# Tap work of a convolution pinned behind the newest weight load and conversion of its queue (hybrid MLA and Mamba-2 trunk, one core)

## The chip, the cores and the metric

The kernel runs on one core of one Trainium2 chip. The metric is device time in microseconds, the median of several runs. Engines are named as in the profile: PE is TensorE (PEld its weight loads), DVE is VectorE, ACT is ScalarE, POOL is GpSimd, and SP is the sync engine, which issues most DMAs.

## The reference, cut to what matters

Two layers: an MLA mixer with an MLP, and a Mamba-2 (SSM) mixer with an MLP, on 256 tokens of width 2048 in float32. The change touches only the SSM mixer:

```python
zxbcdt = h @ w_in                                  # 2048 x 10304
z, xbc, dt = split(zxbcdt)
xbc = silu(causal_depthwise_conv(xbc, conv_w, conv_b))   # width 4, along the tokens
xs, b_in, c_in = split(xbc)                        # 4096, 1024, 1024 channels
...
cb = einsum('blgn,bsgn->blsg', c_c, b_c)           # scores of a group, masked by decay
y_diag = einsum('blsgh,bsghp->blghp', cb[..., None] * decay, x_c)
y = (y_diag + d_skip * xs) * silu(z)               # then a norm per group, then @ w_out
```

There are 8 groups of 8 heads with 64 channels each. The convolution of the x part is `out[t] = sum_i w[i] * x[t - 3 + i] + b`, followed by `silu`.

## The kernel before, in words

**Weights.** All weights come from HBM as float32 in pieces of 128 x 1024 (a *unit*). Each unit is loaded by SP into a raw buffer (`wraw`, 6 buffers, `Flow.fetch`, L87). It is then split into two halves of reduced precision whose sum is the weight: ScalarE writes the high half `wh` (L102), and VectorE writes the low half `wl` as raw minus high (L103), each with 4 buffers. TensorE multiplies with both: for one unit 8 matmuls with `wh` (L325, L326) and then 4 with `wl` (L329). When TensorE's program comes to unit j, `Flow.next` has issued the loads up to j+6 and the conversions up to j+3. `self.last` is the newest high-half conversion that has been issued.

**Order.** `Trunk.block` walks over the keys of a product; one key is two units here, and after each key it calls `tick()`. A function registered with `later(n, fn)` runs at the (n+1)-th tick from then on; in this way the work around the products is spread over the keys. Only TensorE's queue runs in the order of this program. For the other engines and for SP a scheduler draws up the order at compile time with a cost model of its own, taking the program's order as priority among what it holds to be ready; each queue then runs strictly in that order on the chip, and an instruction that has to wait holds back all those behind it. `tc.issue_after(ins)` forces the instructions of a block to stand behind `ins` in the queue of their engine. Before the change only two places of the MLA layer use it.

**The SSM layer** runs its blocks in this order: `B0 d0 C0 x0 B1 x1 C1 x2 z0 x3 z1 x4 z2 o0 x5 z3 x6 z4 o1 x7 z5 z6 o2a z7 o2b o3`. An x block computes the 512 x channels of one group (4 keys, 8 units), a z block its gate, an o block part of the output product. Around them:

- `x_block(g)`: ScalarE copies the product out of PSUM into `x` (tile `xtm`, L1184), and a DMA from ScalarE's queue writes it to a DRAM tensor `xD` (L1185). `shift` reads it back from DRAM at three token offsets into `taps` (128 x 2 x 3 x 512, one buffer for all groups, L1191). `weights` loads the convolution weights and the bias, repeated over the partitions, into `cw` (one buffer, L1176). `mult(t)` multiplies the three shifted copies (L1195) and `x` itself (L1196) by their weights. L1196 overwrites `x`, so it has to wait until the write to `xD` has read it. `total(t)` adds the three taps and the bias (L1200) and then lets ScalarE take a tanh (L1202); `silu(t)` finishes with L1205. t is 0 or 1, one half of the tokens.
- `ahead` hands the group's 8 heads to a queue and starts `across` (two ticks later, L1219, L1221), the part of the second token half that comes from the first. It is the only reader of columns 128 to 255 of `cb[g]`.
- `cb_group(g)`: the scores of a group; VectorE masks the two diagonal parts (L1167), ScalarE copies the unmasked far part (L1168).
- `head`: the decay rows of a head come as `cm` from DRAM (L1246), go through ScalarE (L1250, L1251) and VectorE (L1253); after eight heads the products follow (L1268), then L1271 and L1273 on GpSimd and L1274 on VectorE.
- `z_block`: a tanh (L1288), L1289 on VectorE, then `gate`: L1299 on GpSimd, squares with sums on ScalarE (L296), and L1305 on VectorE.

Of the kernel before, what the change touches and what calls it, by code (L numbers as in the profile page):

```python
# [20 lines left out]
F32 = mybir.dt.float32  # L21
F32R = mybir.dt.float32r
I32 = mybir.dt.int32
AF = mybir.ActivationFunctionType
ALU = mybir.AluOpType
# [3 lines left out]
P = 128  # L29
# [42 lines left out]
class Flow:  # L72
# [8 lines left out]
    def fetch(self, ld, cuts=None, beside=None):  # L81
        n = ld.src.shape[-1]
        ld.tile = self.pools[ld.pool].tile([P, 1024], F32, tag=ld.pool, name=f"w{ld.pool}{self.loaded}")
        for o, z in cuts or ((0, n),):
            if cuts:
                beside()
            self.nc.sync.dma_start(ld.tile[:, o:z], ld.src[:, o:z])  # L87

    def load(self, upto, cuts=None, beside=None):
        while self.loaded < min(upto, len(self.units)):  # L90
# [4 lines left out]
    def halves(self, raw, n, step=None):  # L95

        nc = self.nc
        h = self.pools["wh"].tile([P, 1024], F32R, tag="wh", name=f"wh{self.done}")
        lo = self.pools["wl"].tile([P, 1024], F32R, tag="wl", name=f"wl{self.done}")
        for o in range(0, n, step or n):  # L100
            v = slice(o, o + (step or n))
            self.last = nc.scalar.activation(h[:, v], raw[:, v], AF.Copy)  # L102
            nc.vector.tensor_tensor(lo[:, v], raw[:, v], h[:, v].bitcast(F32), ALU.subtract)  # L103
        return h, lo

    def narrow_halves(self, raw):
# [63 lines left out]
def seven(layer, p, src):  # L170
# [9 lines left out]
    def unit(flow, name, d):  # L180
# [5 lines left out]
        def make():  # L186
            if name == "N7":
                add("b22", "b12", "b22")
                out = halves("b22")
                if d in LATE5:  # L190
                    nc.gpsimd.dma_start(st["b12"].tile, quarter(d, 0, 0), accum_op=ALU.add)
                return out
            if name == "N5" and d not in LATE5:
                add("b12", "b11", "b12")
                return halves("b12")
            if name == "N6":
                add("b11", "b11", "b22")
                out = halves("b11")
                nc.gpsimd.dma_start(st["b11"].tile, quarter(d, 1, 0), accum_op=ALU.add)  # L199
                return out  # L200
            return halves({"M1": "b11", "N4": "b11", "N5": "b12"}.get(name, name))
# [13 lines left out]
class Trunk:  # L215
# [822 lines left out]
    def ssm_body(self, sp, dp, gain):  # L1038
        nc, d, cst = self.nc, self.d, self.cst
# [23 lines left out]
        taps = sp.tile([P, 2, 3, 512], F32, name="taps")  # L1063
        xD = dp.tile([S + 3, GROUPS * 512], F32, name="xD")
# [5 lines left out]

        self.later(1, zeros)

        def conv(ev, ct, dst, lag):

            def half(j):
                b = self.bank(early[0])
                for k in range(2):
                    for t in range(2):
                        o = k * 256 + t * P
                        nc.tensor.transpose(b[:, o:o + P], ev[t][:, (2 * j + k) * P:(2 * j + k + 1) * P], self.ident)  # L1080
                a = self.scratch()
                for k in range(2):
                    c = ct + 2 * j + k
                    wc = lambda i: cst[:, C_CW + 4 * c + i:C_CW + 4 * c + i + 1]
                    s, o = b[:, k * 256:(k + 1) * 256], a[:, k * 256:(k + 1) * 256]
                    nc.scalar.activation(o, s, AF.Identity, bias=cst[:, C_CB + c:C_CB + c + 1], scale=wc(3))
                    for i in (2, 1, 0):
                        m = 3 - i
                        nc.vector.scalar_tensor_tensor(o[:, m:256], s[:, 0:256 - m], wc(i), o[:, m:256], ALU.mult, ALU.add)
                th = self.scratch()  # L1090
                nc.scalar.activation(th, a, AF.Tanh, scale=0.5)
                nc.vector.scalar_tensor_tensor(dst(j), th, 1.0, a, ALU.add, ALU.mult)
            self.later(lag, lambda: half(0))
            self.later(lag + 1, lambda: half(1))
# [9 lines left out]
        def bc_block(name, i):  # L1104
            accs = self.block([("si", name, i, q) for q in range(4)], xT)
            t = self.ktile(self.k4, F32)
            fm[name, i] = t
            conv(evac(accs), (32 if name == "B" else 40) + 4 * i,
                 lambda j: t[:, 2 * j:2 * j + 2].rearrange("p a b -> p (a b)"), 0)
# [50 lines left out]
        def cb_group(g):  # L1160
            B, C = fm["B", g // 4][:, g % 4], fm["C", g // 4][:, g % 4]
            b = self.bank(early[0])
            nc.tensor.matmul(b[:, 0:256], B[:, 0:P], C, start=True, stop=True)
            nc.tensor.matmul(b[:, 256:384], B[:, P:256], C[:, P:256], start=True, stop=True)
            t = sp.tile([P, 384], F32, tag="cb", name=f"cb{g}", bufs=5)
            for o in (0, 256):
                nc.vector.scalar_tensor_tensor(t[:, o:o + P], b[:, o:o + P], 0.125, tri[:, 0:P], ALU.mult, ALU.mult)  # L1167
            nc.scalar.activation(t[:, P:256], b[:, P:256], AF.Copy, scale=0.125)  # L1168
            cb[g] = t

        def x_block(g):
            cw = []

            def weights():
                cw.append(sp.tile([P, 2560], F32, tag="cw", name=f"cw{g}", bufs=1))
                nc.sync.dma_start(cw[0], d["cwx"][g])  # L1176

            self.later(2, weights)
            accs = self.block([("si", "x", g, q) for q in range(4)], xT)
            xt = sp.tile([P, 2, 512], F32, tag="xtm", name=f"xtm{g}", bufs=3)  # L1180
            x = [xt[:, t] for t in range(2)]
            th = [None, None]
            for t in range(2):
                nc.scalar.activation(x[t], accs[t], AF.Copy, scale=rs[t])  # L1184
            nc.scalar.dma_start(xD[3:S + 3, g * 512:g * 512 + 512].rearrange("(t p) n -> p t n", t=2), xt)  # L1185

            def shift():
                for t in range(2):
                    v = xD[t * P:t * P + P, g * 512:g * 512 + 512]
                    row = v.ap[0][0]  # L1190
                    nc.sync.dma_start(taps[:, t], bass.AP(tensor=v.tensor, offset=v.offset, ap=[[row, P], [row, 3], [1, 512]]))  # L1191

            def mult(t):
                flat = taps[:, t].rearrange("p i n -> p (i n)")
                nc.vector.tensor_tensor(flat, flat, cw[0][:, :1536], ALU.mult)  # L1195
                nc.vector.tensor_tensor(x[t], x[t], cw[0][:, 1536:2048], ALU.mult)  # L1196

            def total(t):
                for v in (taps[:, t, 2], taps[:, t, 1], taps[:, t, 0], cw[0][:, 2048:]):
                    nc.vector.tensor_tensor(x[t], x[t], v, ALU.add)  # L1200
                th[t] = self.scratch()
                nc.scalar.activation(th[t], x[t], AF.Tanh, scale=0.5)  # L1202

            def silu(t):
                nc.vector.scalar_tensor_tensor(x[t], th[t], 1.0, x[t], ALU.add, ALU.mult)  # L1205

            def ahead():
                xg[g] = x
                dg = self.gain_tile(d["dsk"][g])
                for i in range(8):  # L1210
                    hq.append((g, i, dg))
                heads_of = lambda v: v.rearrange("p (h f) -> p h f", h=8)
                spread = lambda v: v[:, 8 * g:8 * g + 8].unsqueeze(2).to_broadcast([P, 8, 64])
                xw = self.scratch()
                nc.gpsimd.tensor_tensor(heads_of(xw), heads_of(x[0]), spread(edge[:, 0]), ALU.mult)

                def across():
                    b = self.bank(False)
                    nc.tensor.matmul(b, cb[g][:, P:256], xw, start=True, stop=True)  # L1219
                    far[g] = sp.tile([P, 512], F32, tag="far", name=f"far{g}", bufs=2)  # L1220
                    nc.vector.tensor_tensor(heads_of(far[g]), heads_of(b), spread(edge[:, 1]), ALU.mult)  # L1221

                self.later(1, across)

            self.later(1, shift)
            if g >= 4:
                self.later(0, lambda: cb_group(g))
            self.later(3, lambda: mult(0))
            self.later(4, lambda: total(0))
            self.later(5, lambda: mult(1))  # L1230
            self.later(6, lambda: (silu(0), total(1)))
            self.later(7, lambda: (silu(1), ahead()))

        def pump():
            for _ in range(2 if len(hq) > HEAD_BACKLOG else 1):
# [316 lines left out]
```

## Time and profile before

| | |
|---|---|
| median of 3 runs | 2320.58 us (2319.15 to 2321.26) |
| profiled execution | 2318.87 us, span 2317.1 us |
| granted TensorE clock, mean | 0.999 |
| busy in the span | PE 2291.6, DVE 1922.5, ACT 1387.8, POOL 198.5 us |

A line of the profile names the source line, the engine, the operation and `out<-in` with the names of the tiles; in square brackets stands how long the engine was idle before it and what ended that. A line of the waits reads: who waited, for whom, then microseconds in total, the number of times and the longest. SPq, ACTq and the like are the parts of the engines that issue DMAs.

### The profile page before, as it was taken

What the parts mean: (1) busy time and instruction counts of PE and PEld (TensorE: products, weight loads), DVE (VectorE), ACT (ScalarE), POOL (GpSimd) and SP (SyncE); (2) the same over time, 40 slices, a digit from 0 to 9 for tenths busy, and PEclk for the clock granted to TensorE, in tenths of its full rate; (3) what the DMA queues carried; (4) which work ended last, traced back from release to release, by engine and by line L of the source; (5) the groups of instructions that cost most, each with busy time, mean ns of one, the idle gap of its engine ahead of it and who ended that gap; (6) DMA issues with size and microseconds to landing.
All of it is one profiled execution on the core that took longest, in us unless ns stands there. A gap on an engine that the chain in (4) does not pass through costs nothing. (4 is left out here: it accounts for less than half of the span.)

```text
span 2317.1 us, 30468 instructions
## 1 busy us (share of the span) xinstructions
PE 2291.6 (99%) x10929; PEld 1898.5 (82%) x10929; DVE 1922.5 (83%) x2318; ACT 1387.8 (60%) x1947; POOL 198.5 (9%) x229
## 2 busy tenths in 40 slices
PE   9999999999999999999989999999999999999999
PEld 8888888888888888888777877888888888888887
DVE  7776697899899897678888678676988989989885
ACT  7775466566666656564555555445666656666663
POOL 1430000000000000000121102011000000000000
PEclk9999999999999999999999999999999999999999
DMA  8444687887888878667777777766687788788875
GB/s 314 148 133 149 205 236 243 261 243 244 265 242 252 267 212 265 195 211 251 249 258 237 239 243 249 225 209 193 207 254 236 252 263 242 245 266 242 252 226 165
DMA packets 161912, 538.07 MB, mean 232 GB/s; under 512 B 17680, under 2 KB 26832, under 8 KB 160736
## 3 DMA queue, kind: packets, MB, share of 16 engines
q1 hardware_dynamic: 151264, 502.44, 66.2%
q0 software_dynamic: 8096, 29.41, 7.8%
q10 hardware_dynamic: 2400, 4.27, 0.5%
q8 instruction: 86, 1.41, 0.3%
q14 instruction: 66, 0.54, 0.1%
HBM read 529.65 MB, written 6.41 MB: 231 GB/s over the span
## 5 line engine op out<-in xcount | busy, mean ns | idle before, releaser
L102 ACT ACTIVATE wh<-wraw 128x1024 fp32r<-128x1024 f32 (+1 forms) x818 | 855.0, 1052 | 558.3 <-PE acc L326 215.6
L103 DVE TENSOR_TENSOR wl<-wraw,wh 128x1024 fp32r<-128x1024 f32 (+1 forms) x818 | 988.1, 1223 | 197.6 <-ACT wh L102 189.0
L594 PE MATMUL yp<-wh,k 128*128 128x512 f32 x896 | 350.1, 391 | 0.0
L595 PE MATMUL yp<-wl,k 128*128 128x512 f32 x896 | 349.2, 390 | 0.7 <-DVE wl L103 0.6
L596 PE MATMUL yp<-wh,k 128*128 128x512 f32 x896 | 349.1, 390 | 0.0
L325 PE MATMUL acc<-wh,xt 128*128 128x512 f32 x704 | 280.6, 399 | 4.0 <-ACT wh L102 4.0
L326 PE MATMUL acc<-wh,xt 128*128 128x512 f32 x704 | 275.3, 391 | 0.0
L102 ACT ACTIVATE wh<-wrx 128x1024 fp32r<-128x1024 f32 x168 | 177.9, 1059 | 136.8 <-PE yp L596 107.5
L103 DVE TENSOR_TENSOR wl<-wrx,wh 128x1024 fp32r<-128x1024 f32 x168 | 204.1, 1220 | 37.0 <-ACT wh L102 36.8
L329 PE MATMUL acc<-wl,xt 128*128 128x512 f32 x704 | 190.4, 392 | 10.1 <-DVE wl L103 10.0
L325 PE MATMUL acc<-wh,k 128*128 128x512 f32 x496 | 196.8, 397 | 2.3 <-ACT wh L102 2.2
L595 PEld LDWEIGHTS yp<-wl,k 128*128 128x128 f32 x896 | 168.3, 188 | 35.9 <-DVE wl L103 1.5
L596 PEld LDWEIGHTS yp<-wh,k 128*128 128x128 f32 x896 | 168.2, 188 | 35.0
L594 PEld LDWEIGHTS yp<-wh,k 128*128 128x128 f32 x896 | 168.3, 188 | 34.6
L326 PE MATMUL acc<-wh,k 128*128 128x512 f32 x496 | 193.4, 390 | 0.0
L594 PE MATMUL st<-wh,xt 128*128 128x512 f32 x448 | 177.0, 395 | 0.0
L595 PE MATMUL st<-wl,xt 128*128 128x512 f32 x448 | 174.9, 390 | 0.0
L596 PE MATMUL st<-wh,xt 128*128 128x512 f32 x448 | 174.9, 390 | 0.0
L329 PEld LDWEIGHTS acc<-wl,xt 128*128 128x128 f32 x704 | 131.6, 188 | 41.8 <-DVE wl L103 14.8
L325 PEld LDWEIGHTS acc<-wh,xt 128*128 128x128 f32 x704 | 132.9, 189 | 34.4 <-ACT wh L102 6.1
L326 PEld LDWEIGHTS acc<-wh,xt 128*128 128x128 f32 x704 | 133.0, 189 | 27.9 <-issue 1.2
L199 POOL DMA_DIRECT2D wrx<-mi x56 | 49.1, 876 | 1140.7 <-DVE wl L103 1034.6
(307 smaller groups left out, 3447.7 us busy)
## 6 DMA issues: line engine op xcount, KB each, us to landing
wraw<-mi SPq DMA_DIRECT2D x256, 512.0 KB, 5.2
wraw<-mo SPq DMA_DIRECT2D x256, 512.0 KB, 5.3
wraw<-si SPq DMA_DIRECT2D x160, 512.0 KB, 4.8
wraw<-so SPq DMA_DIRECT2D x64, 512.0 KB, 4.7
wrx<-mi SPq DMA_DIRECT2D x56, 512.0 KB, 5.4
wrx<-mi POOLq DMA_DIRECT2D x56, 512.0 KB, 8.2
wraw<-wo SPq DMA_DIRECT2D x32, 512.0 KB, 3.8
taps<-xD SPq DMA_DIRECT2D x16, 768.0 KB, 7.4
```

Source lines behind the costliest of these rows:

```text
L102: self.last = nc.scalar.activation(h[:, v], raw[:, v], AF.Copy)
L103: nc.vector.tensor_tensor(lo[:, v], raw[:, v], h[:, v].bitcast(F32), ALU.subtract)
L199: nc.gpsimd.dma_start(st["b11"].tile, quarter(d, 1, 0), accum_op=ALU.add)
L325: nc.tensor.matmul(accs[t][:, :n], ah, wh[:, q, :], start=first and kt + q == 0, stop=False)
L326: nc.tensor.matmul(accs[t][:, :n], al, wh[:, q, :], start=False, stop=False)
L329: nc.tensor.matmul(accs[t][:, :n], lhs(kt + q, t)[0], wl[:, q, :], start=False, stop=en and q == nk - 1)
L594: nc.tensor.matmul(b, ah, wh, start=first and q == 0, stop=False)
L595: nc.tensor.matmul(b, ah, wl, start=False, stop=False)
L596: nc.tensor.matmul(b, al, wh, start=False, stop=last and q == 1)
```

## The change

The new helper `behind(what)` opens `tc.issue_after` on the newest weight load (`last_load`), low-half conversion (`last_lo`) or high-half conversion (`last`) that has been issued. With it:

- the tap reads stand behind the newest weight load in SP's queue, and are registered one tick later; the load of `cw` is registered one tick later too
- the products of both token halves are registered for the same tick, behind the newest low-half conversion in VectorE's queue (before: ticks 4 and 6 after the block; now both at tick 5)
- the tanh becomes a function of its own, behind the newest high-half conversion in ScalarE's queue, at ticks 7 and 8 (before: with the sums, at ticks 5 and 7); the sums move from ticks 5 and 7 to 6 and 7, and both silu to tick 8
- the copy of the far score part runs one tick after its group's masked parts, behind the newest high-half conversion

No instruction is added or taken away.

```diff
-            self.nc.sync.dma_start(ld.tile[:, o:z], ld.src[:, o:z])
+            self.last_load = self.nc.sync.dma_start(ld.tile[:, o:z], ld.src[:, o:z])
...
-            nc.vector.tensor_tensor(lo[:, v], raw[:, v], h[:, v].bitcast(F32), ALU.subtract)
+            self.last_lo = nc.vector.tensor_tensor(lo[:, v], raw[:, v], h[:, v].bitcast(F32), ALU.subtract)
...
+        def behind(what):
+            return self.tc.issue_after(getattr(self.flow, what).ins)
...
-            nc.scalar.activation(t[:, P:256], b[:, P:256], AF.Copy, scale=0.125)
             cb[g] = t
+
+            def far_part():
+                with behind("last"):
+                    nc.scalar.activation(t[:, P:256], b[:, P:256], AF.Copy, scale=0.125)
+
+            self.later(0, far_part)
...
-            self.later(2, weights)
+            self.later(3, weights)
...
             def shift():
-                for t in range(2):
+                with behind("last_load"):
+                    for t in range(2):
...
             def mult(t):
                 flat = taps[:, t].rearrange("p i n -> p (i n)")
-                nc.vector.tensor_tensor(flat, flat, cw[0][:, :1536], ALU.mult)
-                nc.vector.tensor_tensor(x[t], x[t], cw[0][:, 1536:2048], ALU.mult)
+                with behind("last_lo"):
+                    nc.vector.tensor_tensor(flat, flat, cw[0][:, :1536], ALU.mult)
+                    nc.vector.tensor_tensor(x[t], x[t], cw[0][:, 1536:2048], ALU.mult)
...
             def total(t):
                 for v in (taps[:, t, 2], taps[:, t, 1], taps[:, t, 0], cw[0][:, 2048:]):
                     nc.vector.tensor_tensor(x[t], x[t], v, ALU.add)
+
+            def tanh(t):
                 th[t] = self.scratch()
-                nc.scalar.activation(th[t], x[t], AF.Tanh, scale=0.5)
+                with behind("last"):
+                    nc.scalar.activation(th[t], x[t], AF.Tanh, scale=0.5)
...
-            self.later(1, shift)
+            self.later(2, shift)
             if g >= 4:
                 self.later(0, lambda: cb_group(g))
-            self.later(3, lambda: mult(0))
-            self.later(4, lambda: total(0))
-            self.later(5, lambda: mult(1))
-            self.later(6, lambda: (silu(0), total(1)))
-            self.later(7, lambda: (silu(1), ahead()))
+            self.later(4, lambda: (mult(0), mult(1)))
+            self.later(5, lambda: total(0))
+            self.later(6, lambda: (tanh(0), total(1)))
+            self.later(7, lambda: (silu(0), tanh(1), silu(1), ahead()))
```

More of the change, by code (lines that the diff above doesn't have):

```diff
@@ L1187, in shift @@
             def shift():
-                for t in range(2):
-                    v = xD[t * P:t * P + P, g * 512:g * 512 + 512]
-                    row = v.ap[0][0]
-                    nc.sync.dma_start(taps[:, t], bass.AP(tensor=v.tensor, offset=v.offset, ap=[[row, P], [row, 3], [1, 512]]))
+                with behind("last_load"):
+                    for t in range(2):
+                        v = xD[t * P:t * P + P, g * 512:g * 512 + 512]
+                        row = v.ap[0][0]
+                        nc.sync.dma_start(taps[:, t], bass.AP(tensor=v.tensor, offset=v.offset, ap=[[row, P], [row, 3], [1, 512]]))
             def mult(t):
                 flat = taps[:, t].rearrange("p i n -> p (i n)")
-                nc.vector.tensor_tensor(flat, flat, cw[0][:, :1536], ALU.mult)
-                nc.vector.tensor_tensor(x[t], x[t], cw[0][:, 1536:2048], ALU.mult)
+                with behind("last_lo"):
+                    nc.vector.tensor_tensor(flat, flat, cw[0][:, :1536], ALU.mult)
+                    nc.vector.tensor_tensor(x[t], x[t], cw[0][:, 1536:2048], ALU.mult)
             def total(t):
```

## The prediction

> **What bounds the kernel now.** I read the page first, then the busy time by stage, then the waits, then the order of time around single stops. The page says that TensorE is the bound: it is busy for nearly the whole span, so only time in which it stands still can be won.
>
> ```profile
> span 2317.1 us, 30468 instructions
> ...
> PE 2291.6 (99%) x10929; PEld 1898.5 (82%) x10929; DVE 1922.5 (83%) x2318; ACT 1387.8 (60%) x1947; POOL 198.5 (9%) x229
> ```
>
> The next view cuts the SSM layer into stages. The three stages left out lost nothing. Columns: stage, its length, then the busy time of each engine, clock, DMA.
>
> ```profile
> core 0: us, PE busy (x) PEld busy (x) DVE busy (x) ACT busy (x) POOL busy (x), PEclk, DMA share, GB/s
> 1017.00:1126.00 109.00, 109.00 (x546) 90.01 (x545) 90.88 (x136) 60.29 (x98) 6.97 (x5) 1.00 0.76 248
> 1126.00:1180.00 54.00, 50.22 (x274) 40.01 (x273) 45.65 (x59) 30.02 (x56) 12.59 (x7) 1.00 0.78 251
> 1180.00:1235.00 55.00, 49.48 (x265) 39.36 (x264) 45.78 (x58) 30.12 (x55) 11.34 (x7) 0.97 0.76 246
> 1235.00:1290.00 55.00, 50.28 (x274) 39.79 (x273) 46.65 (x62) 29.17 (x55) 12.46 (x7) 1.00 0.78 243
> ...
> 1333.00:1382.00 49.00, 47.60 (x214) 38.89 (x213) 42.42 (x58) 27.48 (x39) 5.08 (x4) 1.00 0.76 245
> 1382.00:1436.00 54.00, 51.80 (x281) 40.97 (x279) 44.14 (x58) 24.85 (x45) 12.52 (x7) 1.00 0.74 242
> ...
> 1480.00:1535.00 55.00, 53.83 (x241) 44.04 (x240) 46.38 (x65) 28.65 (x39) 9.30 (x7) 1.00 0.68 216
> ...
> sum 576.00, PE 557.21 PEld 452.61 DVE 450.15 ACT 305.00 POOL 86.01; mean PE 55.72 PEld 45.26 DVE 45.02 ACT 30.50 POOL 8.60
> ```
>
> The sum row covers the whole layer: 576.00 - 557.21 = 18.8 us of idle TensorE, all of it in the last six stages shown. The whole span has 2317.1 - 2291.6 = 25.5 us, so most of what can be won lies here. The waits, restricted to this layer, say on whom TensorE and its weight loads waited and what kept those engines (total, times, longest):
>
> ```profile
> PE acc L329 <- DVE wl L103: 13.3, 14, 2.0
> PE acc L325 <- ACT wh L102: 5.4, 3, 2.2
> ...
> PEld acc L329 <- DVE wl L103: 20.3, 17, 2.5
> PEld acc L325 <- ACT wh L102: 7.8, 7, 2.7
> ...
> DVE xtm L1196 <- DMA xD<-xtm: 27.6, 8, 4.8
> DVE taps L1195 <- DMA taps<-xD: 19.9, 8, 4.2
> ...
> ACT mt L1250 <- DMA cm<-cumD: 35.5, 11, 7.1
> ACT s L296 <- POOL xtm L1299: 34.5, 16, 4.6
> ACT cb L1168 <- DVE cb L1167: 30.0, 6, 8.6
> ACT s L1202 <- DVE xtm L1200: 27.3, 7, 5.4
> ACT wh L102 <- DMA wraw<-si: 21.1, 7, 7.1
> ...
> SPq L1191 <- DMA xD<-xtm: 41.5, 8, 6.3
> ```
>
> TensorE waits only for conversions (L102, L103). These come late because their queues stand behind instructions that wait for something else: on VectorE the tap products (L1195, L1196), on ScalarE the tanh (L1202) and the score part (L1168), on SP the tap read (L1191), which holds back the weight loads behind it. One stop in order of time shows all of it:
>
> ```profile
> 1132.85 0.69 DVE L1196 TENSOR_TENSOR xtm<-xtm,cw 128x512 f32<-128x512 f32 x1 [2.77 <-DMA xD<-xtm]
> 1132.89 0.91 SPq L1191 DMA_DIRECT2D taps<-xD  x2
> ...
> 1139.58 1.76 DVE L1195 TENSOR_TENSOR taps<-taps,cw 128x1536 f32<-128x1536 f32 x1 [2.11 <-DMA taps<-xD]
> ...
> 1141.25 1.22 DVE L103 TENSOR_TENSOR wl<-wraw,wh 128x1024 fp32r<-128x1024 f32 x1
> ...
> 1142.53 1.21 PE L329 MATMUL acc<-wl,xt 128*128 128x512 f32 x4 [0.92 <-DVE wl L103]
> ...
> 1142.92 1.06 ACT L102 ACTIVATE wh<-wraw 128x1024 fp32r<-128x1024 f32 x1 [5.66 <-DMA wraw<-si]
> ```
>
> VectorE loses 2.77 and 2.11 us to DMAs, the conversion ends at 1142.47, TensorE stops; the raw buffers come free late, SP sat behind the tap read, and ScalarE waits 5.66 us for weights.
>
> **What a stop may cost.** From the waits: TensorE idle is 13.3 + 5.4 = 18.7 us, but its weight loads waited 20.3 + 7.8 = 28.1 us, and a restart also costs some tenths, since weight load and matmul no longer overlap. The true loss lies between; I take the middle, 23.4, and 0.6 more for the clock, **24 us**:
>
> ```profile
> 1180.00:1200.00 20.00, 17.10 (x68) 13.06 (x67) 12.41 (x14) 10.79 (x17) 0.00 (x0) 0.94 0.83 267
> ...
> 1197.35 1.76 PE L329 MATMUL acc<-wl,xt 128*128 128x512 f32 x4 [2.04 <-DVE wl L103]
> ```
>
> The clock fell to 0.94 over 20 us, which is 1.2 us; half of it is already inside the middle value, because the slowed matmuls stand as busy. The Trainium skill (TensorE: Matmul & The Clock Gate, "What's actually happening") puts the fall after a window of about 3.4 us without activity; the stop here had 2.04 us, so by that rule there would be no such loss, and the sum would be 0.6 us smaller. The row goes against it.
>
> **The change, part by part.** A step below is one tick (one key of two weight units), counted from the end of an x block. A unit lasts 2.72 us, the pace at which ScalarE is let on:
>
> ```profile
> 1079.52 1.06 ACT L102 ACTIVATE wh<-wraw 128x1024 fp32r<-128x1024 f32 x1 [1.66 <-PE acc L326]
> ```
>
> (1.66 idle + 1.06 busy.) Conversion j+3 may start when unit j-1 is done and must be done three units later, so ScalarE has 3 x 2.72 - 1.06 = 7.1 us of cover; VectorE, whose half is read after eight of the twelve matmuls (1.8 us), 3 x 2.72 + 1.8 - 1.06 - 1.22 = 7.7 us.
>
> *Tap read* (16 DMAs): from step 2 to step 3, and behind the newest weight load. Nothing is added; the 41.5 us in which SP stood still before it should go, since two more loads, each released by a conversion at the pace of 2.72 us, now pass first: 5.4 us against a mean wait of 41.5 / 8 = 5.2. The tap rows come later but are used two steps later. The weight rows cw move one step and are needed five steps on: nothing.
>
> *Tap products*: from steps 4 and 6 in the program (executed from about step 2.5 on) to step 5, behind the newest lo conversion. That takes 27.6 + 19.9 = 47.5 us of waits, 5.9 per group, off VectorE's queue. New: all four come in one go.
>
> ```profile
> L1195 DVE TENSOR_TENSOR taps<-taps,cw x16: 1748/1756/1759, 1041.2 to 1494.6; 128x1536 f32<-128x1536 f32 x16
> ...
> L1196 DVE TENSOR_TENSOR xtm<-xtm,cw x16: 681/689/694, 1034.6 to 1487.1; 128x512 f32<-128x512 f32 x16
> ...
> L1200 DVE TENSOR_TENSOR xtm<-xtm,taps x48: 678/684/689, 1045.1 to 1502.7; 128x512 f32<-128x512 f32 x48
> ```
>
> 2 x 1.76 + 2 x 0.69 = 4.9 us, during which the next L103 waits; its cover is 7.7, so by itself the burst costs nothing. If the conversions are already 3 us late when it starts, TensorE stops again.
>
> *Tanh and score part*: behind ScalarE's newest conversion, tanh at steps 7 and 8 (was 5 and 7), the score part one step later. 30.0 + 27.3 = 57.3 us of waits leave ScalarE's queue, and most of the 21.1 us for late weights. The score part is read by TensorE only eight steps later, tanh by the silu, which now comes at step 8: covered, if the sums are ready by then.
>
> **What remains.** The waits L296 (34.5) and L1250 (35.5) aren't touched. At full cover they cost nothing (the first row: ScalarE stood 3.67 us, and its whole stage, 1480 to 1535, lost 1.2 us); after a queue that was already late they cost a stop (the second):
>
> ```profile
> 1528.01 0.72 ACT L296 ACTIVATE s<-xtm,rs 128x512 f32<-128x512 f32 x1 [3.67 <-POOL xtm L1299]
> ...
> 1269.99 0.50 PE L325 MATMUL acc<-wh,k 128*128 128x512 f32 x1 [2.24 <-ACT wh L102]
> ```
>
> And VectorE stays nearly full: 45.65 / 50.22, 45.78 / 49.48 and 46.65 / 50.28 are 91 to 93% of the time without stops, and the 4.9 us of products and 8 x 0.68 = 5.5 us of sums of a group now fall into steps 5 to 8, where before they began at 2.5. So I leave each of the eight groups 1.3 us, a bit over half of that 2.24: 10.4 us (bounds 0 and 24). Sum: 24 - 10.4 = 13.6 us. The profiled execution took 2318.87 us (span 2317.1 plus 1.8), 1.7 below the median 2320.58 of the runs; 2320.6 - 13.6 = **2307.0 us**. With all 24 gone 2296.6; with 7 gone 2313.6.
>
> **Rivals.**
>
> *VectorE takes over*: the waits go, but the work they leave is packed into steps 5 to 8 and conversions stay late. For it: 93% busy; against it: steps 1 to 4.5 are now free of tap work, so it arrives with full cover. It would give back 17 to 22 of the 24: 2313.6 to 2318.6.
>
> *Slower: the packed taps meet the head rows.* The heads of the group before run around step 8, and there ScalarE waits for cm:
>
> ```profile
> 1175.71 0.40 ACT L1250 ACTIVATE mt<-cm,pcum 128x128 f32<-128x128 f32 x1 [7.08 <-DMA cm<-cumD]
> ...
> 1154.43 3.52 POOL L1299 TENSOR_TENSOR xtm<-s,xtm 128x512 f32<-128x512 f32 x2 [35.27 <-DVE s L1289]
> ...
> 1154.87 1.93 DVE L103 TENSOR_TENSOR wl<-wraw,wh 128x1024 fp32r<-128x1024 f32 x1
> ```
>
> 7.08 is all of ScalarE's cover. If VectorE still has 4 us of sums and silu ahead of the conversion then (today they are over by step 7), TensorE stops for about 7.1 + 4 - 7.7 = 3.4 us in each of eight groups: 27 us back for 24 won plus about 5 where nothing is lost today (the first stage): +8, so 2329. It decides from some 0.6 us of late sums on. Beside GpSimd L103 took 1.93 for 1.22, 0.7 more. The Trainium skill (SBUF: State Buffer, "SBUF: two separate sides") has a VectorE instruction with two SBUF inputs blocked for the whole GpSimd one; by that rule it would lose up to 1.8 here (half of 3.52) and this case would be more likely; the row shows less than half. Against the rival: today the same cm waits meet heads and gate work there and TensorE doesn't stop at 1175.
>
> *No effect*: the pins only name an instruction to follow; if the queue order stays nearly as it is, the time does: 2318 to 2322.
>
> **How the numbers follow.** Forecast 0.62 (its own range 2296 to 2314), VectorE takes over 0.18, no effect 0.06, slower 0.14. About 0.2%, 4.6 us, can be told from no change: faster means under 2316. Half of the second case lies below, and a little more: 0.62 + 0.11 = 0.73 faster, 0.07 + 0.06 = 0.13 same, 0.14 slower. The range 2296 to 2320 holds the first two cases and half of the third.
>
> **What the profile will show.** Right: the waits L1196, L1195, L1168, L1202 and L1191 near zero, those of L102 on wraw under 5 us, idle TensorE in the layer near 8 us, L296 and L1250 as before. Wrong: stops of TensorE on L103 at steps 5 to 9 as long as now, or new ones in the first stage, or tanh waiting for the sums again.

## The result and the profile after

The changed kernel takes 2299.93 us (median of 5 runs, 2298.04 to 2303.34); the kernel before takes 2320.11 (median of 5, 2317.85 to 2321.26). The ratio is 0.9915, 95% interval 0.9901 to 0.9930: 20 us faster. The forecast was 2307.0, range 2296 to 2320. The profiled execution took 2299.97 us.

The page of the changed kernel, its span and TensorE's line:

```profile
span 2298.2 us, 30453 instructions
...
PE 2285.3 (99%) x10929; PEld 1897.3 (83%) x10929; DVE 1908.4 (83%) x2318; ACT 1392.4 (61%) x1947; POOL 213.2 (9%) x229
```

The span fell by 18.9 us: TensorE is idle 12.6 us less (25.5 to 12.9), and 6.3 us less *busy* (2291.6 to 2285.3) with the same 10929 matmuls. The busy part is what matmuls cost above their normal pace, after a restart and at the lower clock (the last section has the numbers). So idle time alone gave two thirds of the gain.

The waits of the changed kernel in the SSM layer, engine by engine. Line numbers have moved: tap products are L1205 and L1206 (were L1195, L1196), sums L1210 (L1200), tanh L1215 (L1202), tap read L1200 (L1191), head rows L1262 (L1250), the gate's product L1311 (L1299) and its last step L1317 (L1305). In some of the runs below the lines of the gate stand one lower or higher.

```profile
PE sm L310 <- DVE s L1317: 5.5, 5, 1.6
PE acc L329 <- DVE wl L103: 0.5, 1, 0.5
...
PEld acc L329 <- DVE wl L103: 1.3, 2, 0.9
PEld acc L325 <- ACT wh L102: 0.7, 3, 0.2
...
SPq L1200 <- DMA xD<-xtm: 7.9, 5, 3.1
...
ACT mt L1262 <- DMA cm<-cumD: 32.8, 13, 7.1
ACT s L1215 <- DVE xtm L1210: 19.5, 12, 4.5
ACT s L296 <- POOL xtm L1311: 14.5, 14, 1.7
...
ACT wh L102 <- DMA wraw<-si: 2.8, 1, 2.8
...
DVE wl L103 <- ACT wh L102: 100.9, 79, 3.2
```

Before, weight loads waited 28.1 us for conversions; now 2.0. VectorE's waits for the tap DMAs are gone, and VectorE now waits longer for ScalarE at its conversions (100.9 us; 57.6 before, both from 1000 to 1600 us of the span), which means that it is ahead of it. What remains is new: TensorE waits 5.5 us for L1317, the last step of the gate on VectorE, whose result it has to transpose (L310). One such place on VectorE:

```profile
1349.37 0.68 DVE L1210 TENSOR_TENSOR xtm<-xtm,taps 128x512 f32<-128x512 f32 x1
...
1350.72 1.28 DVE L1210 TENSOR_TENSOR xtm<-xtm,taps 128x512 f32<-128x512 f32 x2
1351.93 0.74 DVE L1317 SCALAR_TENSOR_TENSOR s<-xtm,st,gb 128x512 f32<-128x512 f32 x1
1352.59 0.68 DVE L1210 TENSOR_TENSOR xtm<-xtm,cw 128x512 f32<-128x512 f32 x1
1353.19 0.74 DVE L1317 SCALAR_TENSOR_TENSOR s<-xtm,st,gb 128x512 f32<-128x512 f32 x1
```

The sums of the convolution stand ahead of and between the two instructions that TensorE waits for. TensorE's row for this place:

```profile
1352.82 0.63 PE L310 MATMUL sm<-cst,s 128*128 128x128 f32 x4 [1.27 <-DVE s L1317]
```

### The profile page after: what moved, and what is told of

The parts are those of the page before. It is cut to its first block, busy times and chain, and to the rows that moved or that the text cites. A ratio compares the mean times of both kernels' runs of the same rounds, so it can differ in the third digit from the quotient of the medians.

```text
span 2298.2 us, 30453 instructions
## 1 busy us (share of the span) xinstructions
PE 2285.3 (99%) x10929; PEld 1897.3 (83%) x10929; DVE 1908.4 (83%) x2318; ACT 1392.4 (61%) x1947; POOL 213.2 (9%) x229
## 4 chain that ended last, share of the span: by engine, by line
PE 94%; DVE 3%; DMA 1%; issue 1%; POOL 1%; ACT 1%; SPq 0%; DVEq 0%; ACTq 0%; POOLq 0%
PE acc L325 12%; PE acc L326 12%; PE acc L329 12%; PE yp L595 9%; PE yp L596 9%; PE yp L594 9%; PE st L595 7%; PE st L596 7%; PE st L594 7%; PE sm L310 2%; DVE wl L103 1%; DMA wraw<-mi 1%; PE acc L594 1%; PE acc L596 1%; PE acc L595 1%
## 5 line engine op out<-in xcount | busy, mean ns | idle before, releaser
L102 ACT ACTIVATE wh<-wraw 128x1024 fp32r<-128x1024 f32 (+1 forms) x818 | 857.9, 1053 | 606.4 <-PE acc L326 290.8
L103 DVE TENSOR_TENSOR wl<-wraw,wh 128x1024 fp32r<-128x1024 f32 (+1 forms) x818 | 984.5, 1218 | 239.0 <-ACT wh L102 228.0
L102 ACT ACTIVATE wh<-wrx 128x1024 fp32r<-128x1024 f32 x168 | 177.9, 1059 | 136.9 <-PE yp L596 105.0
L103 DVE TENSOR_TENSOR wl<-wrx,wh 128x1024 fp32r<-128x1024 f32 x168 | 203.8, 1219 | 37.3 <-ACT wh L102 37.2
L329 PE MATMUL acc<-wl,xt 128*128 128x512 f32 x704 | 188.3, 389 | 0.0
L329 PEld LDWEIGHTS acc<-wl,xt 128*128 128x128 f32 x704 | 132.1, 188 | 27.7
```

The source lines that it names most:

```text
L103: self.last_lo = nc.vector.tensor_tensor(lo[:, v], raw[:, v], h[:, v].bitcast(F32), ALU.subtract)
L329: nc.tensor.matmul(accs[t][:, :n], lhs(kt + q, t)[0], wl[:, q, :], start=False, stop=en and q == nk - 1)
```

## The experiments

Three theories. *VectorE*: the gain comes from tap products that no longer wait for DMAs ahead of conversions. *SP*: it comes from weight loads no longer held back by tap reads. *ScalarE*: it comes from tanh and score part no longer holding back L102. First each part of the change was undone by itself.

### One part undone

SP part undone:

```diff
-                with behind("last_load"):
+                with nullcontext():
-            self.later(3, weights)
+            self.later(2, weights)
-            self.later(2, shift)
+            self.later(1, shift)
```

> The changed kernel with the SP part undone: tap reads one step earlier and unpinned, the weight rows cw one step earlier. The VectorE theory (the gain comes from tap products that no longer stand ahead of conversions while a DMA lands) expects most of the gain kept: 2300 to 2305 us, idle TensorE in the SSM layer under 9 us. The SP theory (the weight loads held behind the tap reads made the conversions late) expects the waits of L102 for wraw back near 20 us and 2310 to 2318. The ScalarE theory (tanh and score part held back L102) expects 2300 to 2303.

VectorE part undone:

```diff
-                with behind("last_lo"):
+                with nullcontext():
-            self.later(4, lambda: (mult(0), mult(1)))
-            self.later(5, lambda: total(0))
+            self.later(3, lambda: mult(0))
+            self.later(4, lambda: total(0))
+            self.later(5, lambda: mult(1))
```

> The changed kernel with the VectorE part undone: tap products unpinned at steps 4 and 6. VectorE theory: the waits of L1195 and L1196 for their DMAs come back (over 30 us in sum) and the time is 2312 to 2320, idle TensorE in the layer 12 to 19 us. SP theory: 2300 to 2305. ScalarE theory: 2300 to 2305.

Tanh undone (no pin, in the step of its sums, silu one step earlier for the first half):

```diff
-                with behind("last"):
+                with nullcontext():
                     nc.scalar.activation(th[t], x[t], AF.Tanh, scale=0.5)
-            self.later(5, lambda: total(0))
-            self.later(6, lambda: (tanh(0), total(1)))
-            self.later(7, lambda: (silu(0), tanh(1), silu(1), ahead()))
+            self.later(5, lambda: (total(0), tanh(0)))
+            self.later(6, lambda: (silu(0), total(1), tanh(1)))
+            self.later(7, lambda: (silu(1), ahead()))
```

> The changed kernel with the tanh back in the step of its sums, unpinned. VectorE and SP theories: 2299 to 2304, since ScalarE has 7 us of cover. ScalarE theory: waits of the tanh for the sums over 25 us, 2308 to 2315.

Score part undone:

```diff
-                with behind("last"):
+                with nullcontext():
                     nc.scalar.activation(t[:, P:256], b[:, P:256], AF.Copy, scale=0.125)
-            self.later(0, far_part)
+            far_part()
```

> The changed kernel with the copy of the far score part back beside its masked parts, unpinned. VectorE and SP theories: 2299 to 2303. ScalarE theory: the wait of this copy for VectorE is back (20 to 30 us over 6 places) and the time is 2303 to 2310.

| undone | us | ratio to before | 95% interval |
|---|---|---|---|
| SP part | 2318.1 | 0.9994 | 0.9985 to 1.0003 |
| VectorE part | 2306.26 | 0.9945 | 0.9928 to 0.9961 |
| tanh | 2355.31 | 1.0154 | 1.0139 to 1.0169 |
| score part | 2300.41 | 0.9920 | 0.9905 to 0.9935 |

No theory foresaw all of this. The SP theory nearly had the time without its part (2310 to 2318), but by waits for `wraw` near 20 us, which did not come. The score part carries nothing that can be measured. Without the SP part the whole gain is gone, without the tanh part the kernel is 36 us slower than before, and without the VectorE part, which I held for the core, 14 of 20 us remain. The waits say why. With the tanh undone, not one stop is left at a conversion; TensorE waits only for the gate:

```profile
PE sm L310 <- DVE s L1317: 50.0, 8, 8.9
```

ScalarE's queue around one of these stops, with the tanh undone:

```profile
1161.58 0.63 ACT L1215 ACTIVATE s<-xtm 128x512 f32<-128x512 f32 x1 [1.37 <-DVE xtm L1210]
1162.12 0.71 ACT L296 ACTIVATE s<-xtm,rs 128x512 f32<-128x512 f32 x1
...
1162.83 0.71 ACT L296 ACTIVATE s<-xtm,rs 128x512 f32<-128x512 f32 x1
```

and, in the changed kernel, at the same z block:

```profile
1146.21 0.73 ACT L296 ACTIVATE s<-xtm,rs 128x512 f32<-128x512 f32 x1 [0.51 <-POOL xtm L1311]
...
1148.44 0.72 ACT L296 ACTIVATE s<-xtm,rs 128x512 f32<-128x512 f32 x1 [1.41 <-POOL xtm L1311]
...
1160.85 0.63 ACT L1215 ACTIVATE s<-xtm 128x512 f32<-128x512 f32 x1 [1.58 <-DVE xtm L1210]
```

With the tanh undone the gate's squares (L296) stand behind the unpinned tanh, and that behind six conversions; in the changed kernel they stand ahead of the tanh. The tanh itself waits only 1.37 us here. What the squares read was ready at 1148.4 us, when L1311 ended on GpSimd, so it is their place in the queue that delays them: they run 14 to 16 us later than in the changed kernel, the gate's last step some 10 us later (1169.32 against 1159.47), and its transposes stop TensorE for 8.86 us. Why the scheduler gave the tanh that place is argued only: it needs sums that come late, because the tap products now start at step 5. With the SP part undone, SP stands 34.1 us before the tap reads, and TensorE again stops at the gate. In one such place head rows land late, ScalarE and VectorE wait one behind the other, and some 20 us later TensorE waits for the gate:

```profile
1198.95 0.99 ACT L1262 ACTIVATE mt<-cm,pcum 128x128 f32<-128x128 f32 x3 [4.36 <-DMA cm<-cumD]
...
1200.28 1.35 DVE L1265 SCALAR_TENSOR_TENSOR mt<-mt,dt,cb 128x128 f32<-128x128 f32 x4 [4.42 <-ACT mt L1263]
...
1222.47 1.09 PE L310 MATMUL sm<-cst,s 128*128 128x128 f32 x4 [6.18 <-DVE s L1317]
```

Weight loads, for which the SP theory spoke, were not late there: L102 waits for `wraw` 3.8 us in that run. That the head rows were late because of the tap reads ahead of them on SP is argued from the order of the queue; no run isolates it.

### One part alone

The same parts put into the kernel before, one at a time; the edits are those above the other way round. The ScalarE part is tanh and score part together. A fourth run tests what remains in the changed kernel:

```diff
-                    self.later(0, lambda t=t: self.transposes(ws[t], yT[g][0], yT[g][1], t, False))
-                self.later(0, lambda: gated.add(g))
+                    self.later(int(g < 5), lambda t=t: self.transposes(ws[t], yT[g][0], yT[g][1], t, False))
+                self.later(int(g < 5), lambda: gated.add(g))
```

> The kernel before with the SP part alone (tap reads one step later behind the newest weight load, cw one step later). Additive theory (each part gives what its undoing costs: SP 18, VectorE 6, ScalarE's tanh 55 us in the other sense): about 2302 us. Chain theory (the parts only work together, because each shifts which of VectorE, ScalarE and the gate's transposes is late): the tap products still stand unpinned and now wait longer for the later taps, so no gain: 2315 to 2330, with the wait of L1195 for the taps above 20 us.

> The kernel before with the VectorE part alone (all four tap products at step 5 behind the newest low half). Additive theory: 6 us faster, 2314. Chain theory: the sums come later while the tanh still stands unpinned ahead of the gate's squares in ScalarE's queue, so the gate is late and its transposes stop TensorE some 8 us in six groups: 2340 to 2365, with nearly no stop on a conversion.

> The kernel before with the ScalarE part alone (tanh and far score part pinned and later). VectorE theory: the DMA waits of L1195 and L1196 remain (about 45 us) and with them most stops: 2310 to 2320. ScalarE theory: most of the gain, 2300 to 2306. Chain theory: as the VectorE theory, with fewer stops on L102 after z blocks: 2308 to 2316.

> The changed kernel with the gate's transposes one step (5.4 us) later for groups 0 to 4; the last three stay, since their results are needed at once. If the remaining idle time of the changed kernel (6 us, nearly all of it transposes that wait for L1317 by up to 1.65 us) is only a matter of that order, it goes for the first five groups and the time falls by 4 to 6 us to 2294 to 2296. If the work is simply too much for VectorE, the stops come back on conversions and the time stays at 2299 to 2301.

| | us | ratio to before | 95% interval |
|---|---|---|---|
| SP part alone | 2319.58 | 0.9995 | 0.9986 to 1.0004 |
| VectorE part alone | 2355.85 | 1.0150 | 1.0133 to 1.0167 |
| ScalarE part alone | 2303.48 | 0.9926 | 0.9911 to 0.9940 |
| changed, transposes a step later | 2300.14 | 0.9911 | 0.9897 to 0.9926 |

The SP part alone gives nothing, as the chain theory said: the tap read no longer waits on SP, but the tanh's waits for the sums grow from 27.3 to 69.6 us. The VectorE part alone is 36 us slower, as the chain theory said too. It takes away every wait of VectorE for the tap DMAs, and loses. The ScalarE part alone gives 17 of the 20 us, which the VectorE and the chain theory both missed: with it, VectorE still waits 39.5 us for the same DMAs, while TensorE is idle only 6.9 us in the layer (18.8 before).

```profile
DVE xtm L1206 <- DMA xD<-xtm: 20.1, 7, 3.6
DVE taps L1205 <- DMA taps<-xD: 19.4, 8, 4.2
```

In the fourth run the waits for L1317 fell from 5.5 to 1.9 us, but a new one of 2.1 us came (a score matmul behind L300) and the time stayed. That left open whether the order on VectorE was the cause.

### What of the ScalarE part, and the rest

Tanh alone; its pin alone, in the old steps; its later step alone, without the pin:

```diff
# tanh_only, against before; tanh_pin has only the pin, tanh_move only the steps
+                with behind("last"):
+                    nc.scalar.activation(th[t], x[t], AF.Tanh, scale=0.5)
-            self.later(6, lambda: (silu(0), total(1)))
-            self.later(7, lambda: (silu(1), ahead()))
+            self.later(6, lambda: (tanh(0), total(1)))
+            self.later(7, lambda: (silu(0), tanh(1), silu(1), ahead()))
```

and the changed kernel with its sums after the gate:

```diff
-            self.later(5, lambda: total(0))
-            self.later(6, lambda: (tanh(0), total(1)))
-            self.later(7, lambda: (silu(0), tanh(1), silu(1), ahead()))
+            self.later(6, lambda: (total(0), total(1)))
+            self.later(7, lambda: (tanh(0), tanh(1), silu(0), silu(1), ahead()))
```

> The kernel before with the tanh part alone: tanh at steps 7 and 8 behind the newest high half, the silu with it; tap reads, tap products and the far score part as before. Tanh theory (what keeps ScalarE late is the tanh that stands ahead of conversions and waits for VectorE's sums): 2302 to 2306, as with the whole ScalarE part (2303.5). Score theory (the far score part, 30 us of waits, carries that gain): 2312 to 2320.

> The kernel before with the tanh pinned behind the newest high half, but in the step of its sums (5 and 7) as before. If the pin carries the gain: 2302 to 2308 and waits of the tanh for the sums under 15 us. If the place in the program carries it: 2312 to 2320, with those waits near 27 us.

> The kernel before with the tanh moved to steps 7 and 8 without the pin. If the pin carries the gain, the scheduler draws the tanh forward again: 2312 to 2320 with waits of 20 us and more. If the place carries it, since the gate's squares then come first by priority: 2302 to 2308.

> The changed kernel with both sums registered one tick after the gate (step 7) and both tanh at step 8. If the remaining waits of the gate's transposes (5.5 us) come from sums that stand ahead of L1317 in VectorE's queue, they go: 2294 to 2297. If the later sums then hold up the tanh, the silu and the heads, the tanh waits over 30 us and the time is 2300 to 2310.

| | us | ratio to before | 95% interval |
|---|---|---|---|
| tanh, pinned and later | 2304.45 | 0.9935 | 0.9920 to 0.9950 |
| tanh, pin alone | 2318.64 | 0.9999 | 0.9990 to 1.0008 |
| tanh, later alone | 2313.22 | 0.9970 | 0.9959 to 0.9981 |
| changed, sums after the gate | 2294.87 | 0.9892 | 0.9877 to 0.9907 |

The tanh alone gives 15 us. Neither half of its edit does: pinned in the old step it still stands ahead of the squares and waits; moved without the pin, 6 of the 15 us come. ScalarE's queue at the second z block shows the difference. The kernel before:

```profile
1199.99 1.25 ACT L1288 ACTIVATE s<-acc,rs 128x512 f32<-128x512 f32 x2
1206.61 0.63 ACT L1202 ACTIVATE s<-xtm 128x512 f32<-128x512 f32 x1 [5.37 <-DVE xtm L1200]
1207.15 1.05 ACT L102 ACTIVATE wh<-wraw 128x1024 fp32r<-128x1024 f32 x1
1211.18 0.72 ACT L296 ACTIVATE s<-xtm,rs 128x512 f32<-128x512 f32 x1 [2.98 <-POOL xtm L1299]
```

With the pin alone:

```profile
1207.01 0.63 ACT L1215 ACTIVATE s<-xtm 128x512 f32<-128x512 f32 x1 [3.56 <-DVE xtm L1210]
1211.58 0.72 ACT L296 ACTIVATE s<-xtm,rs 128x512 f32<-128x512 f32 x1 [3.94 <-POOL xtm L1312]
```

With pin and later step:

```profile
1202.66 0.73 ACT L296 ACTIVATE s<-xtm,rs 128x512 f32<-128x512 f32 x1 [8.74 <-POOL xtm L1312]
...
1205.62 3.88 ACT L102 ACTIVATE wh<-wraw 128x1024 fp32r<-128x1024 f32 x4
1209.40 0.61 ACT L1215 ACTIVATE s<-xtm 128x512 f32<-128x512 f32 x1
```

In the last, the tanh has nothing to wait for, ScalarE stands in one long wait (8.74 us) ahead of the squares, and four conversions follow at once. The wait for late weights fell with it from 21.1 to 11.3 us, though nothing on SP was touched. But the later step alone does all of this too: no tanh waits in that run (it had been expected to wait 20 us and more if the pin carries the gain), the long wait is the same 8.74 us, and late weights cost 9.3 us. What differs is the place of the tanh. With the later step alone one stands ahead of the first conversion, and TensorE, which waits for that conversion, stops longer:

```profile
1206.81 0.61 ACT L1215 ACTIVATE s<-xtm 128x512 f32<-128x512 f32 x1
1207.33 1.04 ACT L102 ACTIVATE wh<-wraw 128x1024 fp32r<-128x1024 f32 x1
1208.28 0.61 ACT L1215 ACTIVATE s<-xtm 128x512 f32<-128x512 f32 x1
...
1208.42 0.50 PE L325 MATMUL acc<-wh,xt 128*128 128x512 f32 x1 [2.25 <-ACT wh L102]
```

With pin and later step the stop at this place is shorter:

```profile
1206.71 0.50 PE L325 MATMUL acc<-wh,xt 128*128 128x512 f32 x1 [1.76 <-ACT wh L102]
```

So the later step takes away the tanh's waits, and the pin takes the tanh itself out of the conversions' way. TensorE's idle time in the layer is 18.8 us before, 17.6 with the pin alone, 10.3 with the later step alone and 5.8 with both. That the half microsecond at such places adds up to the 9 us between the last two runs is not shown.

With the sums after the gate, TensorE no longer waits for the gate at all, as was expected if the order on VectorE was the cause (the edit also moves the first tanh one step). This is what is left in the layer:

```profile
PE acc L329 <- DVE wl L103: 0.5, 2, 0.3
```

and on VectorE both L1317 (here L1316) now stand ahead of most sums:

```profile
1156.27 1.22 DVE L103 TENSOR_TENSOR wl<-wraw,wh 128x1024 fp32r<-128x1024 f32 x1
1157.41 1.41 DVE L1316 SCALAR_TENSOR_TENSOR s<-xtm,st,gb 128x512 f32<-128x512 f32 x2
1158.73 1.22 DVE L103 TENSOR_TENSOR wl<-wraw,wh 128x1024 fp32r<-128x1024 f32 x1
1159.87 2.49 DVE L1210 TENSOR_TENSOR xtm<-xtm,taps 128x512 f32<-128x512 f32 x4
```

At 2294.87 us it is the fastest version, 5 us below the changed kernel by the medians. Their intervals against before, 0.9877 to 0.9907 and 0.9901 to 0.9930, overlap a little, and the two were not run side by side.

## Why the prediction was right or wrong

- *TensorE stops at conversions and nowhere else, and the layer is worth some 24 us.* Right. 18.9 us of span won and 6.0 us of idle time left in the layer make 24.9. To take the middle between idle time and weight-load waits held. The clock term in it was read too small: its window ends at 1200 us, but the clock stayed at half until 1201.1, which is 1.7 us and not 1.2.
- *What remains: 10.4 us, at conversions.* The mis-sized term. At conversions next to nothing remained (weight loads wait 2.0 us). Some 6 us remain at a place that I did not name, the gate's transposes behind the sums. That is most of the difference between 13.6 forecast and 18.9 won in the profiled executions. That the remainder is of a like size at another place, and the time therefore inside the range, is in part luck.
- *Tap products: 5.9 us per group leave VectorE's queue.* True as a wait, but not where the gain was: with the tanh alone, 36.5 of these 47.5 us remain and 15 us are won; with the VectorE part alone all leave and 36 us are lost. The step that failed is to take these waits, by their totals, for a reason of the late conversions: with the tanh alone the longest is 4.3 us, less than the 7.7 us of cover that the prediction itself counts, and TensorE is idle 5.8 us.
- *Tap read: 41.5 us on SP should go.* They went to 7.9. Alone that gave nothing; in the whole change the SP part (with the load of `cw`) is worth 18 us, and with it undone TensorE stopped at the gate, not at weights; the link through the head rows is argued only.
- *Tanh: covered.* Of the four totals of waits that I listed the tanh's was the smallest, and its part carries most: the tanh stood ahead of conversions and of the gate's squares. Its waits did not go to zero as I said (27.3 to 19.5 us), which I had named as a sign of being wrong; what changed is what stands behind it. L296, which I held to be untouched, fell from 34.5 to 14.5.
- *Score part.* It stood in the same entry as the tanh, with 30 us of waits, and was worth 0.5 us or nothing in the changed kernel. Undoing it there brought back only 5.9 us of these waits; with the tanh alone 26.8 us of them remain, and the ratio, 0.9935, is not clear of the 0.9926 of the whole ScalarE part.
- *The slower rival, packed taps that meet later work,* was right in kind and wrong in place. Packed taps without the pinned tanh are 36 us slower, by the gate's chain and not by head rows at step 8. What kept it from happening was the part that I had costed at nothing.
- *Clock.* Right that a stop can lower it, but one of 17 did in the kernel before: after the stop of 2.04 us it was at half for 3.4 us, while after stops of 2.01 and 2.24 us it stayed at 1.00. What decides this is open. Long stops lowered it too: with the VectorE part alone the layer ran at a mean of 0.96, with stops of up to 8.8 us. The Trainium skill (TensorE: Matmul & The Clock Gate, "What's actually happening") asks for a window of about 3.4 us without activity; the row of before, 0.94 after a stop of 2.04 us, disagrees.
- *GpSimd beside a conversion.* Misread. The prediction sets the 0.7 us that L103 lost against half of 3.52 us. But that row holds two instructions, of 1.29 and 2.27 us, and of the first only 0.85 us were left when L103 began. So the row does not speak against a full block by one instruction.

Open: whether in the changed kernel the pin or the step of the tanh is the needed half, and how far the tanh's place ahead of conversions explains that the later step alone wins only 6 us. Every edit also shifts the order that the compiler's scheduler draws up elsewhere, and the parts are not additive; the runs show which order each kernel had, not why the scheduler chose it.

## What to carry to other kernels

A long wait in a queue costs only if what stands behind it runs out of cover, so ask of each waiting instruction which later ones it holds back and who waits for those; the total of a wait says little. When work is moved later, follow its consumer on every other queue and pin it behind what must not wait, in the same edit: half of such a change can be worse than none. When a stop disappears, look which instruction is next to be late, and reorder against it.

## What was not expected of the hardware

The write of 512 KB to DRAM and its reading back take long: in the kernel before a median of 6.6 us to landing for the write (5.3 to 9.1) and 7.4 for each of the two tap reads of a group (768 KB), where the DMA engines were busy three quarters of the time. What they take beside idle DMA engines no run here shows.

And TensorE's *busy* time hid a third of what was won: with the same matmuls it fell by 6.3 us. A smaller part of this is the clock. In the kernel before it was at half from 1197.7 to 1201.1 us, which costs 1.7 us; in the changed kernel it did not fall in this layer. At half clock starts are 0.43 us apart, where 0.23 is normal (the kernel before, three matmuls in order of time, after the stop at 1197.35):

```profile
1198.91 0.63 PE L325 MATMUL acc<-wh,xt 128*128 128x512 f32 x1
1199.33 0.63 PE L326 MATMUL acc<-wh,xt 128*128 128x512 f32 x1
1199.76 0.63 PE L325 MATMUL acc<-wh,xt 128*128 128x512 f32 x1
```

The rest, some 4.6 us, lies outside of that fall. Rows behind other stops show where it can come from, though it was not added up: four matmuls of L329 took 1.20 us at 1162.67, after a stop of 0.76 us, where four without a stop take 1.07.
